# Two gaps of 128 bytes in on-chip memory, and four orders of the feed-forward's products

## The chip, the cores and the metric

The program runs on one core of a Trainium2 chip. The metric is device time in microseconds (us), from the first to the last instruction and a little around them; lower is better. The median of three runs of the kernel before is 1766.66 us.

## The reference

One layer of a hybrid diffusion backbone over 256 latent tokens and 256 context tokens of 2048 channels, in float32. What matters here is that nearly everything is a product of 256 (or 512) token rows with a large weight matrix:

```
h  = rmsnorm(x) * (1 + sc1) + sh1                    # and hc, of the context
na_q, na_k, na_v, dn_qkv, dn_z, ..., ft, sg_u, sg_v = split(h @ w_in)
y  = sum_i sigmoid(h @ w_gate[i] + b_gate[i]) * (branch_i @ w_branch[i])   # 4 branches
x  = x + g1 * (y @ w_out)
h  = rmsnorm(x) * (1 + sc2) + sh2
x  = x + g2 * ((silu(h @ w1) * (h @ w3)) @ w2)       # D_FF = 5632
```

## The kernel before

**Exact products in three parts.** A weight block of 256 rows and 512 columns (a "half block", two k tiles `j` = 0, 1 of 128 rows) arrives by DMA in a tile `raw`. ScalarE rounds it to float32r (`whi`, L392), VectorE forms the rest (`wlo = raw - whi`, L394). The activations are held as two such parts too: `hH`/`hL` (the normalised rows; later `h2H`/`h2L` in the same place), `hcH`/`hcL` (context), `yna`, `yft`, `yst`, `ydn` (branch outputs), `mT` and `m8` (the merged rows), `uH`/`uL` (feed-forward). A product is xH·whi + xL·whi + xH·wlo.

**One matmul.** `PE.matmul(acc, x, w)` takes 128x128 numbers of the activation as the stationary operand (the weight load, PEld LDWEIGHTS in the profile) and 128x512 numbers of `whi` or `wlo` as the moving one, and adds to `acc`, an accumulator in PSUM. Every matmul has its own load, so the stationary operand of the next matmul is read while the moving operand of this one streams.

**One half block.** `half_block` (L413 to L426) makes 12 matmuls: for the two token tiles in turn (two accumulators), xH with `whi` (j = 0, 1), xL with `whi` (0, 1), xH with `wlo` (0, 1). `half_blocks` (L442) does the same for a few half blocks with the token tiles outermost. The input projection's first part (L696) has its own loop, over latent tiles (`hH`) and context tiles (`hcH`) by turns.

**Stages.** Up to about 245 us: norms, modulation and the blocks that need the context (L696). Up to about 930 us: other projections, gates and branch products, with the mixers' small work in between. Up to about 1020 us: output projection (stationary `mT`, `m8`). Then the feed-forward: `w1`, `w3` (stationary `h2H`/`h2L`, 11 blocks `f`), and from 1513.5 us `w2` (stationary `uH`/`uL`, four column blocks `cbk`).

**What sets the order.** Class `Issue` merges lanes of side work into one program order around the weight stream, by a coarse model; `half_block` tells it of 0.64 us after each three matmuls (`iq.pe`). Every engine then issues in program order.

**Where tiles lie.** Pools are laid out in the order in which they are opened, each tile at an offset in bytes within a partition: `raw`, three `whi` of 4,096 bytes, three `wlo` of 4,096, the small tiles (1,024 in all), then the long-lived ones: `cb` (8,192), `hH`, `hL` (16,384 each), `kdn`, `vdn` (8,192 each), small ones (384 in all), and behind these the pools that come and go with the stages (`y8`, `hc`, `mT`, `u`). Slices of a tile by token tile, k tile or `j` start a multiple of 512 bytes into it.

Of the kernel before, what the change touches and what calls it, by code (L numbers as in the profile page):

```python
# [10 lines left out]
F32 = mybir.dt.float32  # L11
# [8 lines left out]
P = 128  # L20
D = 2048
T = 256
# [9 lines left out]
# columns of the packed per-channel parameters  # L32
C_BADA, C_N1, C_N2, C_CONV, C_QN, C_KN = 0, 96, 112, 128, 188, 189
NCOLS = 190
# columns of the constant matrices
M_ID, M_EF, M_EB, M_BD = (128 * i for i in range(4))
NMATS = 512
# how far ahead of its place in the program the weight stream is scheduled
AHEAD = 3000
CFG = {'cvpos': 3, 'cv': 0, 'qv': 0, 'dn': 0, 'ev': 2000, 'evp': 0, 'evx': 0, 'evf': 0, 'evA': 0, 'ahead': 3000, 'adahp': 0, 'proj': {7: 2, 4: 2, 5: 2, 6: 2, 8: 2, 9: 2}, 'gate': {2: 1, 3: 1, 0: 1, 1: 3}, 'wout': [4, 4, 4, 0], 'hopp': 0.2, 'hopb': 0.25, 'hop': 0.2, 'win': 0.5, 'eps': 0.1, 'nz': 1, 'ndn': 11, 'nout': 4, 'groups': [[0, 2], [2, 2], [4, 2], [6, 2], [8, 2], [10, 2], [12, 2], [14, 2]], 'pe': [1, 18], 'pa': 5, 'atail': 8, 'nproj': 2, 'ngate': [9, 0, 8], 'start': 'a0 s0 x0 x1 s1 a16 w0 a1 a17 x2 w1 x3 w2 w3 s2 s3 s4', 'px1': 2, 'psp': 3, 'hoppA': 0.25, 'winA': 0.5, 'winA0': 1, 'hopA': 0.1, 'cw': [0, 0], 'ph1': 1, 'pseed': 0, 'pevac': 1, 'slack': 0.5}  # L40
# groups of k tiles in which the first blocks of the input projection are accumulated
# [7 lines left out]
def _ada_on_pe(t):  # L49
    """Which tiles of the modulation matrix TensorE reduces (the others: VectorE)."""  # L50
    return t in PE_ADA


class Event:
    """A point of the program; t is its time in Issue's model once it has been reached."""
# [5 lines left out]
class Issue:  # L61
    """Merges lanes of work into one program order around the weight stream on TensorE.

    A lane is a generator. It yields, before an operation, the engine ("P", "V", "A" or "G") and about
    how long it holds it (for ScalarE also the function table), or ("wait", event), ("set", event) or
    ("delay", us). Operations are traced when a coarse model of the engines says that their inputs
    are there and their engine is free, so that no engine's queue is blocked by one that comes too early.
    """
# [74 lines left out]
    def stall(self, *events):  # L143
        """Trace other work until the events are reached."""
        for ev in events:
            for _ in range(100000):
                if ev.t is not None:
                    break
                self.now += 0.1
                self.pump()  # L150
            assert ev.t is not None
            while self.now < ev.t:
                self.now = min(ev.t, self.now + 0.3)
                self.pump()
# [10 lines left out]
def build(ctx, tc, A, dbg=None):  # L165
# [12 lines left out]
    hip = ctx.enter_context(pool("hi", 3))  # L178
    lop = ctx.enter_context(pool("lo", 3))
# [19 lines left out]
    def mean_rsqrt(out, in_, scale):  # L199
        """out = (scale * in_ + eps) ** -0.5"""  # L200
        S.activation(out, in_, AF.Sqrt, bias=epsc, scale=scale)
        V.reciprocal(out, out)

# [14 lines left out]
    first_inst = len(nc.cur_bb.bb.instructions)  # L218
    iq = Issue()
# [5 lines left out]
    def pin():  # L225
        """Every engine issues its instructions in program order."""
        last = {}
        for inst in list(nc.cur_bb.bb.instructions)[first_inst:]:
            if inst.engine in last:
                tc.add_manual_dep(inst, last[inst.engine], mybir.DependencyInfo(  # L230
                    mybir.DependencyClass.NoSync, mybir.DependencyReason.DATA), reason="program order")
            last[inst.engine] = inst.name
# [9 lines left out]
    # the stream from memory in the order of use: weights (by k tiles and blocks of 512 columns),  # L242
    # tiles of the modulation matrix in between
# [50 lines left out]
    state = {"k": 0}  # L294
# [108 lines left out]
    def acc_pair():  # L403
        """Two accumulators, and the events that their readers set."""
        res = []
        for _ in range(2):
            if len(accs_free) >= 4:
                iq.stall(accs_free[-4])
            accs_free.append(Event())
            res.append((acc_tile(), accs_free[-1]))  # L410
        return [r[0] for r in res], [r[1] for r in res]

    def half_block(accs, xs, kt0, start, stop, seeded=False):  # L413
        """accs[i] += x_i[:, kt0..]^T @ the next half block of the stream; xs: (hi, lo, token offset)."""
        k = state["k"]
        state["k"] += 1
        iq.stall(split_done[k])
        hi, lo = halves[k]
        for acc, (xh, xl, off) in zip(accs, xs):
            seq = [(xh, hi, j) for j in range(2)] + [(xl, hi, j) for j in range(2)] + [(xh, lo, j) for j in range(2)]  # L420
            for n, (xx, ww, j) in enumerate(seq):
                PE.matmul(acc, xx[:, kt0 + j, off:off + P], ww[:, j], start=start and n == 0 and not seeded,  # L422
                          stop=stop and n == 5, skip_group_check=seeded)
                if n % 3 == 2:
                    iq.pe(0.64)
        mm_done[k].t = iq.now  # L426

    def half_blocks(accs, xs, kts, n0, ready, done, cut=1):
        """Some half blocks from n0 on of an accumulation over eight, one accumulator after the other,
        the very last one in cut parts of its columns."""  # L430
# [80 lines left out]
    def c_lane():  # L511
        """silu(c) as columns, and on every partition as a row, for both streams."""
# [24 lines left out]
    def x_lane(s_, u):  # L537
        """One token tile, scaled to unit root mean square, in the groups of its use."""
# [38 lines left out]
    def mods_lane():  # L577
        """Shift and scale of the normalised rows, by k tile: h = (x * r) * a1 + sh."""
# [13 lines left out]
    def h_lane(s_, parts, banks):  # L592
        """The modulated rows, transposed, as exact float32r parts."""
# [29 lines left out]
    def seed_lane(gi, b, tt, slot):  # L623
        """The accumulator of one output tile; later groups of k tiles start from the sum so far."""
# [32 lines left out]
    # (block, half block, token tile, k tile in it); the first group by token tiles, as they arrive  # L657
# [26 lines left out]
    for gi, (k0, gn) in enumerate(GROUPS):  # L684
        k_first, n_q = state["k"], gn // 2
        state["k"] += 4 * n_q
        for b, q, tt, j in order[gi]:
# [17 lines left out]
            if (b, tt) == (0, 3) and last:  # L705
                # decay / beta columns: both parts of the weights beside each other
# [45 lines left out]
    # gated delta rule: convolutions, norms and decays  # L752
# [11 lines left out]
    def conv_head(src, h, ns, which, room):  # L764
        """Five-tap centred conv along the tokens, per stream, of one head; channels on partitions."""
# [33 lines left out]
    def decay_lane():  # L799
        # decays: g = -exp(a_log) * softplus(a + dt_bias), running sums inside a tile, per direction  # L800
# [35 lines left out]
        # the running sums as rows, for the differences between tokens  # L836
# [25 lines left out]
    # neighbourhood attention: every grid row is a key row (four rows, window of eight)  # L862
# [3 lines left out]
    def na_norm(src, n, dst, wc, x, done):  # L866
        """Root-mean-square norm over the head's channels, and the transpose."""
# [75 lines left out]
    # Fourier mixing  # L943
# [3 lines left out]
    def ft_lane():  # L947
# [9 lines left out]
        for g in range(4):  # L957
            # cosines of rows 0 .. T/2 and sines of rows 1 .. T/2 - 1; the other rows mirror them
# [22 lines left out]
    # spatial gating  # L981
# [48 lines left out]
    # blocks of 128 tokens: B'[j, i] = beta_j (k_j . k_i) exp(gc_i - gc_j), the masked q . k products  # L1030
    def dn_stage(dp):
# [24 lines left out]
        def qv_lane():  # L1056
            room = (lambda n: dp.tile([P, 2 * (T + 4)], F32, name=n, tag={"pad": "l20", "cv": "l21"}[n]), 1)
            # q stays unnormalised (its l2 factor scales the output rows)
# [65 lines left out]
        def sub_lane():  # L1124
            # inverses of the 32 x 32 diagonal blocks by substitution, one block a partition
# [42 lines left out]
        def level(d, tt):  # L1168
            """Blocks of 64, then 128:  V <- V - V (M o B') V"""
# [10 lines left out]
            # (first, second) blocks of a pair, in the order of the recurrence  # L1180
# [41 lines left out]
        # the scan, over tiles of 128 tokens: context first, then latent  # L1222
# [114 lines left out]
    def request_gate(key):  # L1337
        """Reserve the next two accumulators for a gate."""
        gate_waits[key] = accs_free[-4:-2]
        accs_free.extend((Event(), Event()))  # L1340
        gate_accs[key] = [None, accs_free[-2:]]
        gate_wanted[key].t = iq.now

    def bias_lane():
        """A gate's accumulators start from its bias."""
# [61 lines left out]
    def row_lane(dst, rows, m0, done):  # L1407
        """16 modulation columns as one row on every partition."""
# [71 lines left out]
    # gated rmsnorm of the delta rule's output  # L1480
# [115 lines left out]
    def xn_lane(tt):  # L1596
        """Rows of one token tile, scaled to unit root mean square."""
# [16 lines left out]
    def h2_lane(parts, b):  # L1614
        """The modulated rows, transposed, as exact float32r parts, by pairs of k tiles."""
# [24 lines left out]
    # half blocks that stay for both token tiles, one tile after the other  # L1640
# [56 lines left out]
    for f in range(NF):  # L1697
        u_done[f] = Event()
        a1_, f1 = acc_pair()
# [38 lines left out]
    for cbk in range(4):  # L1738
# [4 lines left out]
        xs = [(ff["uH"], ff["uL"], 0), (ff["uH"], ff["uL"], P)]  # L1743
        for f in range(NF):
# [14 lines left out]
def _blocks(w):  # L1759
    """[K, N] -> [N/512, K/512, 128, 4, 512]: each block is one contiguous load."""  # L1760
# [23 lines left out]
def _window():  # L1784
    """Additive column-window mask and the table positions of the attention bias."""
# [61 lines left out]
```

## Time and profile before

| | |
|---|---|
| three runs, us | 1766.38, 1766.66, 1768.25 |
| span of the profiled execution, us | 1764.7 |
| TensorE busy | 1716.4 us (97%), 8297 matmuls |
| VectorE, ScalarE, GpSimd busy | 69%, 54%, 8% |
| 128x512 matmuls with `whi`, `wlo` or `late` as moving operand | 6798 |

The profiled execution's own time outside its span is not listed; the runs lie 1.7 to 3.6 us over the span. [...]

### The profile page before, as it was taken

The numbers are of one execution on the slowest core, as the hardware profiler recorded it, in microseconds if no ns is written. First come the engines' busy times: TensorE is split into PE (matmuls) and PEld (weight loads), VectorE is DVE, ScalarE is ACT, GpSimd is POOL, SyncE is SP. The second block draws the span as 40 slices with busy tenths as digits, with TensorE's granted clock in tenths as the row PEclk, the third lists the DMA queues.
The fourth block names the chain that finished last, engine by engine and source line by source line (L and its number), as shares of the span: only waits on it lengthen the run. The fifth ranks groups of instructions, "written<-read, shape, count | busy, mean of one in ns | idle before, by whom it ended". The sixth has DMA issues, their size and how long they took to land.

```text
span 1764.7 us, 21765 instructions
## 1 busy us (share of the span) xinstructions
PE 1716.4 (97%) x8297; PEld 1398.3 (79%) x8297; DVE 1213.0 (69%) x1522; ACT 950.1 (54%) x1329; POOL 140.5 (8%) x136
## 2 busy tenths in 40 slices
PE   3999999999999999999999999999999999999998
PEld 2777888788778877988888878888888888888887
DVE  5899988885989865767877665565555555544444
ACT  5799987755556566235544474444444444333332
POOL 1000001100211153211101000000000000000000
PEclk9999999999999999999999999999999999999999
DMA  8677787657775755468777645666666655555552
GB/s 322 230 254 256 262 330 260 235 201 253 268 255 177 233 189 198 173 240 297 291 275 266 253 148 211 238 237 239 238 238 238 262 188 188 182 197 190 202 201 107
DMA packets 62461, 406.94 MB, mean 231 GB/s; under 512 B 7730, under 2 KB 8546, under 8 KB 16786
## 3 DMA queue, kind: packets, MB, share of 16 engines
q1 hardware_dynamic: 56164, 386.43, 59.8%
q0 software_dynamic: 4464, 16.49, 3.3%
q10 hardware_dynamic: 1728, 2.62, 0.4%
q8 instruction: 65, 1.06, 0.2%
q14 instruction: 40, 0.33, 0.0%
HBM read 401.29 MB, written 4.23 MB: 230 GB/s over the span
## 4 chain that ended last, share of the span: by engine, by line
PE 62%; issue 2%; POOL 1%; DMA 1%; ACT 0%; DVE 0%; POOLq 0%; ACTq 0%; DVEq 0%
PE acc L422 57%; PE acc L442 2%; POOL l L1175 1%; DMA raw<-w_gate 1%; PE ps L1692 1%; PE ps L1267 0%; POOL mg L1384 0%; PE ps L1256 0%; PE ps L1306 0%; PE ps L1209 0%; PE ps L1216 0%; PE ps L1278 0%; PE ps L1284 0%; PE ps L1288 0%; PE ps L1548 0%
## 5 line engine op out<-in xcount | busy, mean ns | idle before, releaser
L394 DVE TENSOR_TENSOR wlo<-raw,whi 128x1024 fp32r<-128x1024 f32 x532 | 667.0, 1256 | 429.2 <-ACT whi L392 425.6
L392 ACT CAST whi<-raw 128x1024 fp32r<-128x1024 f32 x532 | 558.6, 1052 | 583.9 <-PE acc L422 513.8
L422 PE MATMUL acc<-whi,hL 128*128 128x512 f32 x704 | 230.6, 398 | 0.0
L422 PE MATMUL acc<-whi,hH 128*128 128x512 f32 x704 | 224.5, 400 | 3.2 <-ACT acc L1359 2.6
L422 PE MATMUL acc<-wlo,hH 128*128 128x512 f32 x704 | 218.6, 392 | 2.9 <-DVE wlo L394 2.7
L422 PE MATMUL acc<-whi,h2L 128*128 128x512 f32 x684 | 213.5, 391 | 0.0
L422 PE MATMUL acc<-whi,h2H 128*128 128x512 f32 x684 | 211.7, 391 | 0.0
L422 PE MATMUL acc<-wlo,h2H 128*128 128x512 f32 x684 | 210.7, 389 | 0.0
L369 DVE SCALAR_TENSOR_TENSOR raw<-raw,cb 128x2048 f32<-128x2048 f32 x64 | 151.7, 2373 | 17.9 <-DMA raw<-w_ada 17.8
L422 PEld LDWEIGHTS acc<-wlo,hH 128*128 128x128 f32 x704 | 131.7, 188 | 32.6 <-DVE wlo L394 5.8
L422 PEld LDWEIGHTS acc<-whi,hL 128*128 128x128 f32 x704 | 132.4, 188 | 28.0 <-issue 0.7
L422 PEld LDWEIGHTS acc<-whi,hH 128*128 128x128 f32 x704 | 128.4, 189 | 30.1 <-ACT acc L1359 3.0
L422 PEld LDWEIGHTS acc<-wlo,h2H 128*128 128x128 f32 x684 | 128.4, 188 | 26.6
L422 PEld LDWEIGHTS acc<-whi,h2L 128*128 128x128 f32 x684 | 128.4, 188 | 26.6
L422 PEld LDWEIGHTS acc<-whi,h2H 128*128 128x128 f32 x684 | 127.6, 188 | 26.1
L422 PE MATMUL acc<-whi,uL 128*128 128x512 f32 x340 | 106.8, 395 | 0.0
L422 PE MATMUL acc<-whi,uH 128*128 128x512 f32 x340 | 106.7, 395 | 0.0
L422 PE MATMUL acc<-wlo,uH 128*128 128x512 f32 x340 | 106.5, 394 | 0.0
L357 DVE SCALAR_TENSOR_TENSOR junk<-raw,cb 128x2048 bf16<-128x2048 f32 x30 | 68.5, 2282 | 11.0 <-ACT cb L521 11.0
L422 PEld LDWEIGHTS acc<-whi,uL 128*128 128x128 f32 x340 | 64.1, 188 | 14.9
L422 PEld LDWEIGHTS acc<-wlo,uH 128*128 128x128 f32 x340 | 64.1, 188 | 14.9
L422 PEld LDWEIGHTS acc<-whi,uH 128*128 128x128 f32 x340 | 64.0, 188 | 14.9
(390 smaller groups left out, 2170.9 us busy)
## 6 DMA issues: line engine op xcount, KB each, us to landing
raw<-w SPq DMA_DIRECT2D x132, 1024.0 KB, 4.8
raw<-w_ada SPq DMA_DIRECT2D x96, 1024.0 KB, 5.9
raw<-w_gate SPq DMA_DIRECT2D x64, 1024.0 KB, 4.8
raw<-w_in SPq DMA_DIRECT2D x24, 1024.0 KB, 5.7
raw<-w_in SPq DMA_DIRECT2D x32, 512.0 KB, 5.4
raw<-w_branch SPq DMA_DIRECT2D x16, 1024.0 KB, 4.9
raw<-w_out SPq DMA_DIRECT2D x16, 1024.0 KB, 4.9
bg<-b_gate POOLq DMA_DIRECT2D x16, 256.0 KB, 4.3
```

The costliest lines, as they stand in the source:

```text
L357: V.scalar_tensor_tensor(junk, raw, 1.0, cb, ALU.mult, ALU.mult, accum_out=modA[:, 0, t:t + 1])
L369: V.scalar_tensor_tensor(raw, raw, 1.0, cb, ALU.mult, ALU.mult, accum_out=mod[:, t:t + 1])
L392: S.copy(hi, raws[e][:, 2 * q:2 * q + 2])
L394: V.tensor_tensor(lo, raws[e][:, 2 * q:2 * q + 2], hi.bitcast(F32), ALU.subtract)
L422: PE.matmul(acc, xx[:, kt0 + j, off:off + P], ww[:, j], start=start and n == 0 and not seeded, stop=stop and n == 5, skip_group_check=seeded)
L442: PE.matmul(acc[:, cs], xx[:, kt0 + j, off:off + P], ww[:, j, cs], start=n0 + n + i == 0, stop=n0 + n == 7 and i == 5, skip_group_check=c > 0)
L1175: G.tensor_tensor(dst.rearrange("p h (b i) -> p h b i", b=4), src[:, u0:u0 + 4].unsqueeze(2).to_broadcast([P, 4, 4, 32]), mats[:, M_BD:M_B ...
L1692: PE.transpose(tp[:, P * h:P * h + P], us[tt][:, P * h:P * h + P], ident)
```

## The change

Two tiles of 128 bytes, never written, are put into the layout: `gap0` between `whi` and `wlo`, `gap1` in front of the long-lived tiles. Everything behind them moves up. Offsets modulo 512 bytes, as the allocator gives them:

| tile | before | after |
|---|---|---|
| `raw`, `whi` | 384 | 384 |
| `wlo` | 384 | 0 |
| `hH`, `hL`, `h2H`, `h2L` | 384 | 128 |
| `hc`, `y` tiles, `m8`, `uH`, `uL` | 256 | 0 |
| `mT`, `late` | 160 | 416 |

In `half_block` the order of the 12 matmuls follows `state["mode"]`, which is 0 (the order before) until the feed-forward; there it is `f % 4` for `w1` and `w3` and `cbk` for `w2`. Mode 1 goes by j, with xH·whi, xH·wlo, xL·whi; mode 2 by j, with xH·whi, xL·whi, xH·wlo; mode 3 keeps the order of mode 0 but takes both accumulators in turn at each product. `half_blocks` is unchanged. Comments are removed as well, so L422 becomes L433, L1692 becomes L1703.

```
+    pad0 = ctx.enter_context(pool("pad0")).tile([P, 32], F32, name="gap0")
     lop = ctx.enter_context(pool("lo", 3))
...
+    pad1 = ctx.enter_context(pool("pad1")).tile([P, 32], F32, name="gap1")
     hp = ctx.enter_context(pool("h"))
...
-        for acc, (xh, xl, off) in zip(accs, xs):
-            seq = [(xh, hi, j) for j in range(2)] + [(xl, hi, j) for j in range(2)] + [(xh, lo, j) for j in range(2)]
-            for n, (xx, ww, j) in enumerate(seq):
-                PE.matmul(acc, xx[:, kt0 + j, off:off + P], ww[:, j], start=start and n == 0 and not seeded,
-                          stop=stop and n == 5, skip_group_check=seeded)
-                if n % 3 == 2:
-                    iq.pe(0.64)
+        mode = state.get("mode", 0)
+        seq = [(xh_, ww, j) for xh_, ww in ((0, hi), (1, hi), (0, lo)) for j in range(2)]
+        if mode == 1:
+            seq = [(xh_, ww, j) for j in range(2) for xh_, ww in ((0, hi), (0, lo), (1, hi))]
+        if mode == 2:
+            seq = [(xh_, ww, j) for j in range(2) for xh_, ww in ((0, hi), (1, hi), (0, lo))]
+        todo = [(a, n) for a in range(len(accs)) for n in range(6)]
+        if mode == 3:
+            todo = [(a, n) for n in range(6) for a in range(len(accs))]
+        for i, (a, n) in enumerate(todo):
+            which, ww, j = seq[n]
+            off = xs[a][2]
+            PE.matmul(accs[a], xs[a][which][:, kt0 + j, off:off + P], ww[:, j], start=start and n == 0 and not seeded,
+                      stop=stop and n == 5, skip_group_check=seeded)
+            if i % 3 == 2:
+                iq.pe(0.64)
...
     for f in range(NF):
         u_done[f] = Event()
+        state["mode"] = f % 4
...
         xs = [(ff["uH"], ff["uL"], 0), (ff["uH"], ff["uL"], P)]
+        state["mode"] = cbk
```

The numbers in the names of the next rows tell buffers apart (`acc_8924` and `acc_8925` are the two accumulators). TensorE, the third half block of `w1` at f = 1, before:

```order
L422 MATMUL acc_8924<-whi_8930,h2H_8421 128x512 x2
L422 MATMUL acc_8924<-whi_8930,h2L_8422 128x512 x2
L422 MATMUL acc_8924<-wlo_8931,h2H_8421 128x512 x2
L422 MATMUL acc_8925<-whi_8930,h2H_8421 128x512 x2
L422 MATMUL acc_8925<-whi_8930,h2L_8422 128x512 x2
L422 MATMUL acc_8925<-wlo_8931,h2H_8421 128x512 x2
```

The same half block after (mode 1):

```order
L433 MATMUL acc_8932<-whi_8938,h2H_8429 128x512
L433 MATMUL acc_8932<-wlo_8939,h2H_8429 128x512
L433 MATMUL acc_8932<-whi_8938,h2L_8430 128x512
L433 MATMUL acc_8932<-whi_8938,h2H_8429 128x512
L433 MATMUL acc_8932<-wlo_8939,h2H_8429 128x512
L433 MATMUL acc_8932<-whi_8938,h2L_8430 128x512
L433 MATMUL acc_8933<-whi_8938,h2H_8429 128x512
L433 MATMUL acc_8933<-wlo_8939,h2H_8429 128x512
L433 MATMUL acc_8933<-whi_8938,h2L_8430 128x512
```

`wlo` is now wanted by the second matmul, where it was the fifth, and `whi` and `wlo` follow each other more often. TensorE, a half block of `w2` in the last column block, before:

```order
L422 MATMUL acc_13096<-whi_13363,uH_8775 128x512 x2
L422 MATMUL acc_13096<-whi_13363,uL_8776 128x512 x2
L422 MATMUL acc_13096<-wlo_13364,uH_8775 128x512 x2
L422 MATMUL acc_13097<-whi_13363,uH_8775 128x512 x2
L422 MATMUL acc_13097<-whi_13363,uL_8776 128x512 x2
L422 MATMUL acc_13097<-wlo_13364,uH_8775 128x512 x2
```

The same half block after (mode 3):

```order
L433 MATMUL acc_13104<-whi_13371,uH_8783 128x512
L433 MATMUL acc_13105<-whi_13371,uH_8783 128x512
L433 MATMUL acc_13104<-whi_13371,uH_8783 128x512
L433 MATMUL acc_13105<-whi_13371,uH_8783 128x512
L433 MATMUL acc_13104<-whi_13371,uL_8784 128x512
L433 MATMUL acc_13105<-whi_13371,uL_8784 128x512
L433 MATMUL acc_13104<-whi_13371,uL_8784 128x512
L433 MATMUL acc_13105<-whi_13371,uL_8784 128x512
L433 MATMUL acc_13104<-wlo_13372,uH_8783 128x512
L433 MATMUL acc_13105<-wlo_13372,uH_8783 128x512
```

The accumulators take turns, and `whi` runs for eight matmuls, `wlo` for four. On TensorE nothing else changes place, and the other engines' instructions stand in the same order as before.

## Rows read from the trace of the kernel before

**Rows 1.** The page: span, busy time by engine, the chain that ended last.

```profile
span 1764.7 us, 21765 instructions
PE 1716.4 (97%) x8297; PEld 1398.3 (79%) x8297; DVE 1213.0 (69%) x1522; ACT 950.1 (54%) x1329; POOL 140.5 (8%) x136
...
PE acc L422 57%; PE acc L442 2%; POOL l L1175 1%; DMA raw<-w_gate 1%; PE ps L1692 1%; PE ps L1267 0%; POOL mg L1384 0%; PE ps L1256 0%; PE ps L1306 0%; PE ps L1209 0%; PE ps L1216 0%; PE ps L1278 0%; PE ps L1284 0%; PE ps L1288 0%; PE ps L1548 0%
```

**Rows 2.** The page's groups of matmuls: count | busy us, mean ns | idle us before.

```profile
L422 PE MATMUL acc<-whi,hH 128*128 128x512 f32 x704 | 224.5, 400 | 3.2 <-ACT acc L1359 2.6
L422 PE MATMUL acc<-whi,h2H 128*128 128x512 f32 x684 | 211.7, 391 | 0.0
```

**Rows 3.** Windows, L422 on TensorE: us, busy (matmuls), granted clock.

```profile
1165.00:1200.00 35.00, 35.00 (x156) 1.00 0.71 265
1650.00:1685.00 35.00, 35.00 (x152) 1.00 0.55 200
```

**Rows 4.** TensorE timeline: start us, length, tiles, matmuls; first and last rows of stretches.

```profile
46.53 0.39 PE L696 MATMUL acc<-wlo,hH 128*128 128x512 f32 x1
...
1164.80 0.61 PE L422 MATMUL acc<-wlo,h2H 128*128 128x512 f32 x2
...
1199.71 0.62 PE L422 MATMUL acc<-whi,h2L 128*128 128x512 f32 x2
...
1513.01 0.62 PE L422 MATMUL acc<-wlo,h2H 128*128 128x512 f32 x2
1513.47 0.64 PE L422 MATMUL acc<-whi,uH 128*128 128x512 f32 x2
1513.95 0.62 PE L422 MATMUL acc<-whi,uL 128*128 128x512 f32 x2
...
1519.93 0.62 PE L422 MATMUL acc<-whi,uH 128*128 128x512 f32 x2
...
1559.90 0.39 PE L422 MATMUL acc<-wlo,uH 128*128 128x512 f32 x1
```

**Rows 5.** Line L422, 1165 to 1200 us: count, duration ns min/median/max.

```profile
L422 PE MATMUL acc<-whi,h2H x52: 389/389/389, 1165.3 to 1199.5; 128*128 128x512 f32 x52
```

**Rows 6.** Line L422, 1525 to 1700 us.

```profile
L422 PE MATMUL acc<-wlo,uH x252: 390/393/404, 1525.0 to 1699.6; 128*128 128x512 f32 x126
```

**Rows 7.** Line L696, 200 to 250 us: latent and context by turns.

```profile
L696 PE MATMUL acc<-whi,hL x28: 387/389/398, 200.6 to 237.9; 128*128 128x512 f32 x28
L696 PE MATMUL acc<-whi,hcL x28: 390/393/404, 203.4 to 240.7; 128*128 128x512 f32 x28
```

**Rows 8.** Tiles mT and yft, 240 to 1100 us.

```profile
L422 PE MATMUL acc<-whi,mT x120: 392/395/483, 928.7 to 1004.2; 128*128 128x512 f32 x120
L422 PE MATMUL acc<-whi,yft x64: 390/395/481, 533.8 to 626.4; 128*128 128x512 f32 x64
```

**Rows 9.** Line L422, the one matmul at 796.2 us, at 1395.8 and at 333.2.

```profile
L422 PE MATMUL acc<-wlo,hH x1: 397/397/397, 796.0 to 796.0; 128*128 128x512 f32 x1
L422 PE MATMUL acc<-wlo,h2H x1: 388/388/388, 1395.6 to 1395.6; 128*128 128x512 f32 x1
L422 PE MATMUL acc<-wlo,hH x1: 400/400/400, 333.0 to 333.0; 128*128 128x512 f32 x1
```

**Rows 10.** Line L711: loads and matmuls of a stationary tile used twice running.

```profile
L711 PEld LDWEIGHTS ps<-hH,wabr x16: 187/188/192, 59.6 to 223.1; 128*128 128x128 f32 x16
L711 PEld LDWEIGHTS ps<-hL,wabr x16: 187/188/189, 59.8 to 223.2; 128*128 128x128 f32 x16
```

**Rows 11.** Timelines of VectorE and TensorE: wlo, the feed-forward's u, its transposes.

```profile
1155.60 1.23 DVE L394 TENSOR_TENSOR wlo<-raw,whi 128x1024 fp32r<-128x1024 f32 x1 [1.50 <-ACT whi L392]
1156.75 0.68 DVE L1686 TENSOR_TENSOR us<-us,acc 128x512 f32<-128x512 f32 x1
...
1159.54 0.60 PE L1692 MATMUL ps<-mats,us 128*128 128x128 f32 x4
```

**Rows 12.** Waits of TensorE, 250 to 1513 us: for whom, us, times, longest.

```profile
PE acc L422 <- DVE wlo L394: 2.7, 3, 1.6
```

## The prediction, made before the changed kernel ran

> **What bounds the kernel now.** I read the page's head first: TensorE is busy 97% of the span, and one line, the matmul of the half blocks (L422), makes 57% of the chain that ended last [rows 1]. VectorE and ScalarE have room. From 250 us to the end of w3 the longest single cause for which TensorE waits is `wlo`, 2.7 us in three waits [rows 12]. So the time is the number of matmuls times their pace, and the change touches nothing else: no engine gets an instruction more or less, and only TensorE's order differs.
>
> The pace is read from start to start. In a quiet stretch of w1 and w3, 154 matmuls lie between the rows at 1164.80 and 1199.71 us: 34.91 / 154 = 226.7 ns each. In w2, 172 lie between 1519.93 and 1559.90: 39.97 / 172 = 232.4 ns [rows 4]. [...] The change comes at one point: pairs start 0.45 us apart until `uH` takes the place of `h2H`, and 0.48 us apart with the first pair of w2 [rows 4]. The durations show it matmul by matmul: 389 ns each time with `h2H` [rows 5], 390 to 404 with `uH` [rows 6]. It isn't the stage: in the first part latent and context tiles alternate, and the median is 389 with `hL` and 393 with `hcL`, under the same `whi` [rows 7]. With `mT` and `yft` no matmul is below 390, the medians are 395 [rows 8].
>
> What these tiles differ in is where they lie. I call **distance** the offset of the next stationary tile minus that of the moving one, modulo 512 bytes, since the next weights are read while this matmul streams. From the layout's table: `h` and `h2` have 0 against `whi` and `wlo` alike, context, branch and `u` tiles and `m8` 384, `mT` 288. Distance 0 is the quiet pace, 384 and 288 are not. Slices start a multiple of 512 bytes into a tile, so the distance doesn't change inside a tile.
>
> **The change part by part.**
>
> *The gaps.* They shift `wlo` by 128 bytes and all behind it by 256. The new distances: `h` tiles 256 against `whi` and 128 against `wlo`; context, branch, `u` tiles and `m8` 128 against `whi` and 0 against `wlo`; `mT` 32 and 416; the `late` tiles as before. No `h` tile is at 0 any more. Which of the new distances stalls?
>
> For 256 one row speaks: at 796.2 us a small weight load at distance 256 (16 columns of `mod`) follows a quiet stretch, and the matmul over it takes 397 ns, 8 over the quiet 389; the same instruction at 1395.8 us, at distance 448, leaves its matmul at 388 [rows 9]. So 256 stalls, by one sample and a short load. For 128 there is no row. Its neighbours are 0 (nothing) and 192, where the one at 333.2 us takes 400 ns, 11 over [rows 9]. The bounds for 128 are thus 0 and 11 ns; I take it as stalling, at the sustained 5.7 ns, since all the full-width cases off 0 that run on for long (288 and 384) do [rows 6, 8].
>
> The sum, then. The matmuls with `h` stationary are 3 x 704 and 3 x 684 at L422 [rows 2] and 384 at L696. Of them 3,380 now run at the quiet pace, counted as those whose successor starts 226 or 227 ns later, the first at 46.53 us, the last at 1513.01 [rows 4]; 1,665 of these are in w1 and w3. The others stand behind transposes and small work and are off that pace already. 3,380 x 5.7 ns = 19.3 us lost, if all go to w2's pace. Its spread: if only the two thirds with `whi` pay, 12.9 us; at `mT`'s pace (median 395, 6 over 389) it is 3,380 x 6.5 = 22 us. TensorE waits little after 250 us [rows 12], so nearly all of this is on the path; I take 1 us off for waits on side lanes that get shorter.
>
> What comes back: 1,910 matmuls with context, branch, `u` and `m8` tiles pay 5.7 ns now, 10.9 us in all, 1,034 of them in w2. After the change a third of them, those over `wlo`, are at 0. But a stalled stretch doesn't turn quiet at once: behind the switch from context to latent tiles the first few still take more than 389, up to 398 [rows 7], and with two `wlo` matmuls at a time (one in modes 1 and 2, four in mode 3) there is hardly a stretch long enough. I put it at 0, bounds 0 and 3.6 us gained.
>
> *The orders.* (a) They could change the pace only through the switches from `whi` to `wlo`; that is in the numbers above. (b) Mode 1 has the same stationary tile twice running, 280 times. At L711, where that happens now, each matmul has a load of its own, 16 and 16 [rows 10]; so no load falls away, and 0. (c) Mode 3 changes the accumulator with every matmul. Now it changes with every sixth, and in the quiet stretch all 52 are at 389 [rows 5]: 0, both ways. (d) Modes 1 and 2 want `wlo` three matmuls earlier at most, 0.7 us. VectorE makes it in 1.23 us, itself waiting for ScalarE's `whi` [rows 11], and L422 waits for it three times only, none in the feed-forward [rows 12]: the third buffer hides this. Without that cover it would be 0.7 us a half block, but I see no such place. (e) In mode 3 the first accumulator of a pair is done five matmuls later, 1.1 us. VectorE's product `us` started at 1156.75 us and took 0.68 [rows 11]; its transposes stood at 1159.54 [rows 11], 2.1 us after its end, so 1 us is left: 0.
>
> *VectorE* reads `raw` and `whi`, unmoved, and writes `wlo` 128 bytes further. No row shows it with `wlo` elsewhere. I take 0; 10% either way (0.12 of the 1.23 us, [rows 11]) is far less than the room under (d), and VectorE is 69% busy in all [rows 1].
>
> [...]
>
> **The rivals.**
> 1. *Offsets are not the cause* (some other property of the tiles decides). Then all stays, 1766.7. For it: distance and tile go together in this trace, so a property of the tile would look the same. Against: `hc` and `hH` are made by the same code and differ by place alone. 11%. [...]
> 2. *Faster: both 128 and 256 are quiet.* What stalls might be only a band around 288 to 384. Then `h` keeps its pace, and the 1,910 others come down to it: 1766.7 - 10.9 = 1755.8. It decides in w2, where 1,034 x 5.7 = 5.9 us of it lie: the point is whether `uH` over `whi`, at 128, starts 227 ns apart. Against: the 397 at distance 256. 12%.
> 3. *128 is quiet, 256 is not.* `u`, branch and context tiles become quiet altogether (-10.9), `h` pays over `whi` (+12.9 to +19.3): 1769 to 1775. 12%.
> 4. *Worse: each switch between `whi` and `wlo` sets the pace back*, and the matmuls pay the 11 ns of the single sample at 192 rather than 5.7: 3,380 x 11 = 37 us, 1804. 5%.
>
> **How the numbers follow.** The forecast (60%) is that `h` loses its quiet pace and the others don't gain: 1766.7 + 19.3 - 1 = 1785 us, about 1,783 on the profile's own span of 1764.7. Its own range is 1779 to 1789 (the 12.9 and 22 us from above). Rivals 1 and 3 (23%) lie below, and with them the range reaches from 1764 to 1792; out of it are rival 2, rival 4 and a little of the forecast, about 19%. A difference of 0.2% (3.5 us) is about what a measurement of this kernel can tell from none. Faster: rival 2, 12%. The same: rival 1, 11%. Slower: the forecast, rivals 3 and 4, 77%.
>
> **What would show it.** In the changed kernel's trace: matmuls with `h2H` of w1 and w3 at 390 to 404 rather than 389, pairs 0.465 us apart; w2 as now, about 232 ns; f = 0, 1, 2, 3 alike within 1 ns; no new wait of TensorE. If w1 and w3 stand at 389, I am wrong on 256 (rival 2) or on the cause (rival 1), and w2's durations tell which: 389 there is rival 2, 393 is rival 1. If w2 alone is quiet, it is rival 3. If the four modes differ by more than 2 ns, the switches matter by themselves, and rival 4 or a gain that I have left out is at work.

## The result, and the profile after

The changed kernel takes 1776.65 us (median of four runs, 1774.91 to 1784.58) against 1766.52 for the kernel before beside it: a ratio of 1.0075, with a 95% interval of 1.0051 to 1.0100. It is slower, by 10.1 us on the median and by 8.4 us between the two profiled executions (spans 1773.1 and 1764.7). The page of the changed kernel, to be held against [rows 1] and [rows 2] (span; busy us, share, count; then groups with busy us and mean ns of one):

```profile
span 1773.1 us, 21729 instructions
PE 1725.7 (97%) x8297; PEld 1395.4 (79%) x8297; DVE 1212.4 (68%) x1522; ACT 949.7 (54%) x1329; POOL 139.4 (8%) x136
...
L433 PE MATMUL acc<-whi,h2H 128*128 128x512 f32 x684 | 240.7, 395 | 0.0
...
L433 PE MATMUL acc<-whi,hH 128*128 128x512 f32 x704 | 226.6, 403 | 2.2 <-ACT acc L1370 2.0
...
L433 PE MATMUL acc<-wlo,uH 128*128 128x512 f32 x340 | 116.7, 391 | 0.0
```

The same 8297 matmuls keep TensorE busy 9.3 us longer. The groups with `h2H` and `hH` went from 391 and 400 ns to 395 and 403. (The busy times of the `h2H` group, 211.7 and 240.7 us, can't be compared: overlaps count once within a group, and in the new orders its matmuls seldom follow each other.) VectorE, ScalarE and GpSimd did as much as before. Windows with the matmuls of L433 (us, busy, count, granted clock, DMA share, GB/s), for [rows 3]:

```profile
1165.00:1200.00 35.00, 34.81 (x151) 1.00 0.61 229
1650.00:1685.00 35.00, 35.00 (x155) 1.00 0.55 200
```

In 35 us of w1 and w3 now 151 matmuls run where 156 did, and in w2 155 where 152 did, at a granted clock of 1.00 in all four. TensorE's waits from 250 us to the end of w3 (for whom, us, times, longest), for [rows 12]:

```profile
PE ps L1197 <- POOL l L1186: 3.6, 3, 1.8
PE ps L942 <- DVE rc L937: 2.5, 1, 2.5
PE acc L433 <- ACT acc L1370: 2.0, 1, 2.0
PE acc L433 <- DVE wlo L396: 1.2, 1, 1.2
```

No new wait came; the one for `wlo` fell from 2.7 to 1.2 us, and the one for `l` rose from 2.7 to 3.6. So the loss has to lie in the pace of the matmuls.

**The pace, block by block.** In the quiet stretch of the kernel before, rows 389 ns long start 226.7 ns apart [rows 4, 5], so neighbours overlap; what a matmul costs is read from start to start. These are single rows of the changed kernel's TensorE timeline (start us, length), the first and the last of a stretch of f = 2, of f = 7 and of the second column block of w2, in this order:

```profile
1130.11 0.39 PE L433 MATMUL acc<-whi,h2H 128*128 128x512 f32 x1
...
1158.11 0.39 PE L433 MATMUL acc<-whi,h2H 128*128 128x512 f32 x1
...
1350.04 1.07 PE L433 MATMUL acc<-whi,h2L 128*128 128x512 f32 x4
...
1383.08 1.07 PE L433 MATMUL acc<-whi,h2L 128*128 128x512 f32 x4
...
1600.03 0.39 PE L433 MATMUL acc<-wlo,uH 128*128 128x512 f32 x1
...
1639.17 0.39 PE L433 MATMUL acc<-wlo,uH 128*128 128x512 f32 x1
```

Between them lie 120, 144 and 171 matmuls: 28.00 / 120 = 233.3 ns, 33.04 / 144 = 229.4 and 39.14 / 171 = 228.9. Read so for every block (the mean from start to start of matmuls that follow each other within 260 ns; the kernel before has 227.0 in w1 and w3 by this measure, where its quiet stretch alone has the 226.7 of [rows 4], and 232.4 in w2):

| | mode 0 | mode 1 | mode 2 | mode 3 |
|---|---|---|---|---|
| w1, w3 | 231.3, 231.2, 231.1 (f = 0, 4, 8) | 231.1, 231.1, 231.1 (1, 5, 9) | 233.2, 231.2, 233.2 (2, 6, 10) | 231.3, 229.5 (3, 7) |
| w2 | 231.9 | 229.0 | 229.0 | 232.2 |

Summed over the trace, matmul by matmul against the kernel before: `h` of the first and the middle part (2,203 matmuls) +6.85 us, `h2` (2,052) +8.90, context tiles -0.68, branch tiles -0.35, `u` -1.98, `mT` and `m8` 0.0, and the spaces around waits and small work (all that starts later than 260 ns, or isn't a matmul of this shape), nearly all ahead of the feed-forward, -4.45. Together +8.3 of the 8.4 us.

### The profile page after: what moved, and what is told of

Same layout as the page of the kernel before. It is cut to its first block, busy times and chain, and to the rows that moved or that the text cites. A ratio compares the mean times of both kernels' runs of the same rounds, so it can differ in the third digit from the quotient of the medians.

```text
span 1773.1 us, 21729 instructions
## 1 busy us (share of the span) xinstructions
PE 1725.7 (97%) x8297; PEld 1395.4 (79%) x8297; DVE 1212.4 (68%) x1522; ACT 949.7 (54%) x1329; POOL 139.4 (8%) x136
## 4 chain that ended last, share of the span: by engine, by line
PE 62%; issue 2%; POOL 1%; DMA 1%; ACT 0%; DVE 0%; POOLq 0%; ACTq 0%
PE acc L433 57%; PE acc L453 2%; POOL l L1186 1%; DMA raw<-w_gate 1%; PE ps L1703 1%; PE ps L1278 0%; POOL mg L1395 0%; PE ps L1267 0%; PE ps L1317 0%; PE ps L1220 0%; PE ps L1227 0%; PE ps L1295 0%; PE ps L1289 0%; PE ps L1299 0%; PE ps L1559 0%
## 5 line engine op out<-in xcount | busy, mean ns | idle before, releaser
L433 PE MATMUL acc<-whi,h2L 128*128 128x512 f32 x684 | 240.9, 394 | 0.0
L433 PE MATMUL acc<-whi,h2H 128*128 128x512 f32 x684 | 240.7, 395 | 0.0
L433 PE MATMUL acc<-wlo,h2H 128*128 128x512 f32 x684 | 239.9, 393 | 0.0
L433 PE MATMUL acc<-whi,hL 128*128 128x512 f32 x704 | 232.5, 401 | 0.0
L433 PE MATMUL acc<-whi,hH 128*128 128x512 f32 x704 | 226.6, 403 | 2.2 <-ACT acc L1370 2.0
L433 PE MATMUL acc<-wlo,hH 128*128 128x512 f32 x704 | 220.5, 394 | 1.3 <-DVE wlo L396 1.2
L433 PEld LDWEIGHTS acc<-wlo,hH 128*128 128x128 f32 x704 | 132.3, 188 | 31.7 <-DVE wlo L396 2.8
L433 PEld LDWEIGHTS acc<-whi,hL 128*128 128x128 f32 x704 | 132.8, 189 | 30.1 <-issue 0.7
L433 PEld LDWEIGHTS acc<-whi,hH 128*128 128x128 f32 x704 | 128.3, 188 | 31.3 <-ACT acc L1370 2.4
L433 PEld LDWEIGHTS acc<-whi,h2H 128*128 128x128 f32 x684 | 128.1, 188 | 29.6
L433 PEld LDWEIGHTS acc<-whi,h2L 128*128 128x128 f32 x684 | 128.3, 188 | 29.3
L433 PEld LDWEIGHTS acc<-wlo,h2H 128*128 128x128 f32 x684 | 128.3, 188 | 29.0
L433 PE MATMUL acc<-whi,uL 128*128 128x512 f32 x340 | 117.6, 393 | 0.0
L433 PE MATMUL acc<-whi,uH 128*128 128x512 f32 x340 | 117.2, 393 | 0.0
L433 PE MATMUL acc<-wlo,uH 128*128 128x512 f32 x340 | 116.7, 391 | 0.0
L433 PEld LDWEIGHTS acc<-wlo,uH 128*128 128x128 f32 x340 | 63.8, 188 | 14.5
L433 PEld LDWEIGHTS acc<-whi,uL 128*128 128x128 f32 x340 | 63.9, 188 | 14.4
L433 PEld LDWEIGHTS acc<-whi,uH 128*128 128x128 f32 x340 | 63.7, 188 | 14.5
```

The lines of the kernel that those rows point to most:

```text
L433: PE.matmul(accs[a], xs[a][which][:, kt0 + j, off:off + P], ww[:, j], start=start and n == 0 and not seeded, stop=stop and n == 5, skip_gr ...
```

## The experiments

Distance is used as in the prediction: the offset of the next stationary tile minus that of the moving one. In each of these kernels the whole computation is done. Ratios stand against the kernel before on the same chip.

**One part alone: the four orders** (both gaps taken out of the changed kernel).

```
-    pad0 = ctx.enter_context(pool("pad0")).tile([P, 32], F32, name="gap0")
-    pad1 = ctx.enter_context(pool("pad1")).tile([P, 32], F32, name="gap1")
```

> The four orders in the feed-forward alone, no gaps: every distance is as in the kernel before (0 for h and h2, 384 for u). Distance theory: an order that doesn't change the distance does nothing; w1 and w3 start every 226.7 ns for all f, w2 every 232.4 ns for all four cbk; 1766.5 us, within 3 us. Rival (the orders cost by themselves: the same stationary tile twice running in mode 1, the accumulator changed at each matmul in mode 3): f = 2, 6, 10 at up to 233 ns as in the changed kernel, w1 and w3 some 8 us longer in all, 1770 to 1775 us.

1765.77 us against 1765.76, ratio 0.9999 (0.9983 to 1.0015). w1 and w3 stand at 227.0 ns in every f, whatever its mode, and w2 at 232.4 in all four column blocks. From 1165 to 1200 us, which [rows 5] show in the kernel before (the few longer ones stand around transposes):

```profile
L431 PE MATMUL acc<-whi,h2H x52: 387/389/398, 1164.6 to 1198.4; 128*128 128x512 f32 x52
```

At the constant distances of the kernel before the order costs nothing, and neither `wlo` wanted earlier nor the change of accumulators shows.

**The other part alone: the gaps** (both `state["mode"]` lines taken out).

> The two gaps alone, the order before everywhere. Distance theory: all of w1 and w3 at what f = 0, 4, 8 show in the changed kernel (231.2 ns), all of w2 at what cbk = 0 shows (231.9 ns rather than a mean of 230.5): the changed kernel's time plus 1 to 2 us, 1776 to 1780 us. Rival (the orders make the loss): w1 and w3 at 226.7 ns, at most 1768 us.

1774.92 us, ratio 1.0070 (1.0042 to 1.0097): all of the loss, 1 us under the range that I had expected. w1 and w3 stand at 231.2 in every f, w2 at 231.8 in every column block. From 1165 to 1200 us:

```profile
L433 PE MATMUL acc<-whi,h2H x52: 388/394/473, 1164.8 to 1199.8; 128*128 128x512 f32 x52
```

**The absolute offset or the distance?** A gap in front of `raw` moves every tile by 128 bytes and leaves all distances.

```
+    pada = ctx.enter_context(pool("pada")).tile([P, 32], F32, name="gapa")
     rawp = ctx.enter_context(pool("raw", 3))
```

> 128 bytes in front of raw, so that raw, whi, wlo and everything behind move up together: every offset is new, every distance is that of the kernel before. Distance theory: nothing changes, w1 and w3 at 226.7 ns, w2 at 232.4 ns, span near 1765 us. Rival (the offset of the stationary tile decides, quiet at 384 modulo 512 only): w1 and w3 leave 226.7 ns, as h2 is now at 0.

227.0 to 227.1 and 232.4 ns, as before. The time was 1767.77 in one execution, and 1761.91 for the kernel before beside it, whose executions lie between 1761.3 and 1770.9; so single times say little here, and the paces say it. That all tiles lie 128 bytes further does nothing; how they lie to each other is what counts.

**Every distance 0.** 128 bytes behind the small long-lived tiles bring context, branch and `u` tiles to distance 0, 96 more bring `mT` there; `wlo` and `h` stay.

```
     ab = hp.tile([P, 4, 16], F32, name="ab")
+    padu = hp.tile([P, 32], F32, name="gapu")
...
     dsm = sc.enter_context(pool("dsm"))
+    padm = dsm.tile([P, 24], F32, name="gapm")
```

> The kernel before with 128 bytes behind the h tiles and 96 in front of the merge's tiles, so that every stationary tile (context, branch, u, m8, mT) is at distance 0 from whi and wlo, and h stays there. Distance theory: all quiet stretches at 226.7 ns; 1,910 x 5.7 ns and 190 x 6.4 ns come off, 12 us: 1754.5 us (1752 to 1757). Rival (another property of these tiles makes them slow): w2 stays at 232.4 ns, 1766.5 us.

1753.97 us against 1765.76, ratio 0.9935 (0.9913 to 0.9958). It beats both kernels. Line of the half blocks in w2, 1650 to 1685 us (count, ns min/median/max), where [rows 6] has 390/393/404:

```profile
L423 PE MATMUL acc<-whi,uL x52: 389/389/389, 1649.7 to 1683.9; 128*128 128x512 f32 x52
L423 PE MATMUL acc<-wlo,uH x52: 389/389/389, 1650.1 to 1684.4; 128*128 128x512 f32 x52
```

`u` gained 5.84 us, branch tiles 1.80, context 1.62, `mT` 1.20, `m8` 0.98: 11.4 of the 12.5 us by which its span is shorter (1752.2). The prediction's 10.9 us for these tiles was about right, and the cause, distance, is shown by a gain as well as by a loss. The same matmuls of w2 run at 226.7 ns here and at 232.4 in the kernel before, at a granted clock of 1.00 in both (1535 to 1700 us). By what path the offset acts no run shows.

One more rival: `raw` lies at `whi`'s offset modulo 512, so the party that disturbs could be the transfers into `raw`. The end of w2 in the kernel before speaks against it (us, TensorE busy and count, granted clock, DMA share, GB/s):

```profile
1700.00:1710.00 10.00, 10.00 (x44) 1.00 0.64 238
...
1740.00:1748.00 8.00, 8.00 (x36) 1.00 0.09 36
```

With transfers at 0.64 and at 0.09 of the time the pace is 232.4 ns in both.

**The second gap alone, at four sizes.** `wlo` stays, all long-lived tiles move, so `h` has one distance against `whi` and `wlo` alike. The edit, with 128 bytes, is the diff's `gap1` line; for the others the tile has 64, 48 or 16 elements for 256, 192 and 64 bytes.

> Only the second gap (128 bytes in front of the long-lived tiles), the order before: h and h2 at 128 from whi and wlo alike, context, branch, u and m8 at 0. Distance theory with 128 a stalling distance: w2 at 226.7 ns (-10.9 us with the context and branch tiles), w1 and w3 at 230 to 232.5 ns (+13 to +19 us, less what waits take up): 1768 to 1775 us. Rival (only the alternation of two distances stalls, a constant 128 is quiet): w1 and w3 at 226.7 ns, 1755 us.

128 bytes: 1776.62 us, ratio 1.0064 (1.0045 to 1.0084), 1.6 us over the range that I had expected. `h` and `h2` lost 9.54 + 11.71 = 21.25 us, `u` gained 5.84. The blocks of w1 and w3 show two rhythms for one code and one distance: 233.2 or 233.3 ns for f = 0, 2, 4, 6 and 9, 232.4 for f = 1, 3, 5, 7 and 10 (f = 8 has 232.6). Of f = 3 and f = 4, in this order:

```profile
L423 PE MATMUL acc<-wlo,h2H x50: 390/392/404, 1165.0 to 1199.6; 128*128 128x512 f32 x50
...
L423 PE MATMUL acc<-wlo,h2H x49: 387/396/398, 1210.8 to 1245.2; 128*128 128x512 f32 x49
```

> Only the second gap, 256 bytes wide: h and h2 at a constant 256, context, branch, u and m8 at a constant 128. Theory (every distance but 0 modulo 512 stalls): w1 and w3 at 231 to 233.5 ns; w2 at 232.4 or 233.2 ns, the two paces that h2 showed at 128 with the second gap alone; span 1778 to 1785 us. Rival (the measure is modulo 256, so that 256 is as good as 0, which the 226 ns intervals over whi in the changed kernel's f = 7 suggest): w1 and w3 at 226.7 ns, span near 1765 us.

256 bytes: w1 and w3 stay at 227.0 ns, w2 at 232.4; 1763.33 us in one execution, beside 1761.91. From 1165 to 1200 us:

```profile
L423 PE MATMUL acc<-whi,h2H x52: 389/389/389, 1164.8 to 1199.0; 128*128 128x512 f32 x52
L423 PE MATMUL acc<-whi,h2L x52: 389/389/389, 1165.2 to 1199.5; 128*128 128x512 f32 x52
L423 PE MATMUL acc<-wlo,h2H x52: 389/389/389, 1165.7 to 1199.9; 128*128 128x512 f32 x52
```

These are [rows 5] again, at distance 256. My theory that 256 stalls fell, and its rival, that only the distance modulo 256 counts, came out.

> The second gap, 192 bytes wide: h and h2 at 192, u at 64. Theory (every distance but 0 stalls): both at 230 to 234 ns, span 1778 to 1785 us. Rival (a band around 0 is quiet, 64 in it): w2 at 226.7 ns and w1, w3 slower.

192 bytes: 1768.53 us; `h2` at 192 runs at 228.95 ns, `u` at 64 (modulo 256) at 233.3.

> The second gap, 64 bytes wide: h and h2 at 64, u at 448, which is 64 on the other side of 0. Theory (every distance but 0 stalls): both at 230 to 234 ns, span 1778 to 1785 us. Rival (a band of 64 bytes on either side of 0 is quiet): w1, w3 and w2 all at 226.7 ns, span 1754 us. One-sided: only one of the two is quiet.

64 bytes: 1786.15 us, the slowest of all; `h2` at 64 runs at 233.3 ns, `u` at 192 at 228.9. The roles are exchanged and the paces go with the distance. In both, the tile at 192 is faster than the 230 to 234 ns that I had expected of every distance but 0, and 64 bytes are no quiet band around 0. Durations over `wlo` in both kernels, 1165 to 1200 us, 192 bytes first:

```profile
L423 PE MATMUL acc<-wlo,h2H x50: 388/390/392, 1165.7 to 1198.9; 128*128 128x512 f32 x50
```

```profile
L423 PE MATMUL acc<-wlo,h2H x50: 393/398/405, 1165.1 to 1199.8; 128*128 128x512 f32 x50
```

The map so far, for a stretch in which the distance is constant:

| distance modulo 256 | 0 | 32 | 64 | 96 | 128 | 160 | 192 | 224 |
|---|---|---|---|---|---|---|---|---|
| ns from start to start | 226.7 | 233.1 | 233.3 | 234.2 | 232.4 or 233.2 | 233.4 | 228.9 | 233.3 |
| seen with | `h`, `u` | `mT` | `h`, `u` | `mT` | `h`, `u` | `mT` | `h`, `u` | `mT` |

The values at 96, 160 and 224 are those of `mT` (some 180 matmuls each) in the traces with 64, 128 and 192 bytes. Of all steps of 32 bytes only 0 and 192 are off the slow pace, and 224, nearer to 0 than 192, is on it.

**The first gap alone.** This has the mixed distances of the changed kernel with the roles exchanged: `h` at 128 over `whi` and 0 over `wlo`, `u` at 0 over `whi` and 128 over `wlo`.

```
+    pad0 = ctx.enter_context(pool("pad0")).tile([P, 32], F32, name="gap0")
     lop = ctx.enter_context(pool("lo", 3))
```

> The first gap alone, order as before: wlo and all behind it move by 128 bytes. Distances modulo 256: h tiles 128 over whi and 0 over wlo, context, branch and u tiles and m8 0 over whi and 128 over wlo; the shares of the changed kernel with the roles of h and u exchanged. If the pace follows from the distances of a run of matmuls, whatever tile it is: w1 and w3 at 231.8 ns (the gaps alone have that in w2, where two thirds are at 128 and one third at 0), w2 at 231.2 (theirs in w1 and w3); h loses 3,380 x 5.0 = 17 us, u and its like gain 1,910 x 1.1 = 2 us, about 1780 against 1765. If each matmul paid for its own distance alone: w1 and w3 at 230.5, w2 at 228.6, and 1772.

1776.92 us against 1766.62. w1 and w3 run at 231.8 or 231.9 ns in every f, w2 at 231.1 or 231.2: the paces of the gaps alone, exchanged, so which tile it is doesn't matter, and a matmul doesn't pay for its own distance alone. From 1165 to 1200 us, over `wlo` (distance 0 now) and over `whi` (128):

```profile
L423 PE MATMUL acc<-wlo,h2H x50: 388/395/398, 1164.8 to 1198.9; 128*128 128x512 f32 x50
L423 PE MATMUL acc<-whi,h2H x50: 392/393/479, 1165.3 to 1199.3; 128*128 128x512 f32 x50
```

The matmuls over `wlo` are at distance 0 and yet slower than those at 128: a third or two thirds of quiet distances don't make a quiet stretch. The time lies 3 us under the 1780 that I had expected; `h` lost the 17 us as expected, and the spaces around small work ahead of the feed-forward shrank by 5.0 us in this execution, a term that scatters (see the account of the waits below).

**What the orders do where distances mix.** The changed kernel once more, and both gaps with one order throughout (`state["mode"] = 1`, or 3, at both places).

> The changed kernel once more, for the steadiness of what its trace showed. If the pace follows from distances and order alone, the blocks of w1 and w3 read as in the first trace, one by one: f = 2 and 10 at 233.2 ns from start to start, f = 6, which has the same code and the same distances, at 231.2, f = 7 at 229.5 and f = 3 at 231.3; w2 at 231.9, 229.0, 229.0 and 232.2 in its four column blocks; time 1775. If instead a block settles into one of several rhythms by how it begins, the mean of a mode stays within 229 to 233.5, but the blocks of one mode differ again and not the same ones as before: any of f = 2, 6, 10 may stand at 231.2 or 233.2, and w2's second and third column blocks may leave 229.0; time 1772 to 1780.

Block by block the second execution repeats the first within 0.1 ns: f = 2 and 10 at 233.2, f = 6 at 231.2, f = 7 at 229.5, w2 at 231.9, 229.0, 229.0 and 232.2. So the difference between f = 2 and f = 6, one code and the same distances, isn't chance. (Its time, 1782.26, has another cause, told in the last section.)

> Both gaps, and order 1 in every block of the feed-forward. If the order decides the pace where distances mix: w1 and w3 at 231.1 ns in every f (as f = 1, 5, 9 of the changed kernel), w2 at 229.0 in all four column blocks (as its second one); against the gaps alone (231.2 and 231.8 ns) that is 1,034 x 2.8 ns = 2.9 us less, 1772. If blocks choose their rhythm by how they begin: some f at 233.2 and some column blocks at 231.8, and a time within 2 us of the gaps alone, 1775.

1772.95 us. w1 and w3 at 231.0 to 231.2, w2 at 228.9 to 229.1 in all four column blocks, 2.9 ns under the gaps alone: `u` gained 3.55 us against the kernel before. The sequence has a steady beat of three, of the moving operands `whi`, `wlo` and `whi` (here in w2, 1710 to 1745 us):

```profile
L433 PE MATMUL acc<-whi,uL x52: 391/391/391, 1709.6 to 1744.6; 128*128 128x512 f32 x52
L433 PE MATMUL acc<-whi,uH x52: 393/393/393, 1709.8 to 1744.9; 128*128 128x512 f32 x52
L433 PE MATMUL acc<-wlo,uH x51: 388/388/388, 1710.1 to 1744.4; 128*128 128x512 f32 x51
```

> Both gaps, and order 3 (whi for eight matmuls, wlo for four) in every block of the feed-forward. If the order decides the pace: w1 and w3 alike in every f, at 231.3 or 229.5 ns (the changed kernel's f = 3 and f = 7), w2 at 232.2 in all four column blocks; 1771 to 1775. If blocks choose their rhythm by how they begin: w1 and w3 again show both 231.3 and 229.5 in one run. A third view, that a matmul pays for its own distance alone and order is nothing, would have two thirds at 226.7 and a third at 232.4, 228.6 on the mean for w1 and w3.

1776.1 us. w1 and w3 at 231.4 or 231.5 in every f from 1 on (within 0.2 ns of the changed kernel's f = 3, and 1.9 off its f = 7), w2 at 231.7 in all column blocks; the time lies 1 us over the expected range. With both gaps and one order throughout the blocks agree; in the changed kernel, where the orders alternate, a block of mode 3 stands at 231.3, 229.5 or 232.2. So where distances mix a block's order alone doesn't fix its pace. That what ran before it decides is likely and not shown: f = 2 and f = 6 both follow a block of mode 1 and differ. The view that each matmul pays for its own distance alone (228.6 for w1 and w3) fell here too.

## Why the prediction was right or wrong

The forecast had the right sign and the right cause, and its size was too large: 1785.0, with +19 us, against 1776.65 and +10.1. Point by point:

- **TensorE's pace is the time, and distance sets the pace: right.** The loss is in the gaps alone (1.0070 of 1.0075), and none of it in the orders alone (0.9999). Rival 1, another property of the tiles, fell with every distance at 0, where the same tiles become quiet (w2 at 226.7 ns); the gap in front of all tiles can't speak against it, but shows that the absolute offset is not the cause.
- **"So 256 stalls, by one sample and a short load": wrong, and this is the step that failed.** With 256 bytes all matmuls of the half blocks from 1165 to 1200 us stand at 389, and w1 and w3 at 227.0 ns throughout. The 397 ns of [rows 9] belong to one matmul with a load of 16 columns; it says nothing of full loads. The distance counts modulo 256, not modulo 512: 0 and 256, 128 and 384, 192 and 448 give the same paces (227.0, 232.4 and 228.9 ns, and 233.2 in some blocks at 128).
- **128 stalls, at 5.7 ns: right.** Constant 128 gives 232.4 or 233.2, 5.7 or 6.5 ns over quiet, the forecast's value and the one that I had taken for `mT`'s. Rivals 2 and 3, in which 128 was quiet, fell. What the forecast described, all of `h` stalled, is the second gap of 128 bytes alone: 21.25 us, against the forecast's 19.3 and its upper end of 22.
- **The term of `h`: 19.3 us forecast, 15.75 measured** (6.85 + 8.90). Not all `h` matmuls are at a stalling distance, as I thought, but one third, those over `wlo`. By their own distance alone they would cost a third of 21.25, 7.1 us. The rest, 8.7 us, is the mixture: stalled and quiet distances in turn give 231.2, nearer to the stalled pace than to the quiet one. That a stretch doesn't turn quiet at once, the argument by which I took the gain of `u` as 0, holds for `h` as well. That the term came within 4 us is luck: the mixture, which the sum had for `u` and not for `h`, hides most of the first mistake. (The 1,665 matmuls given for w1 and w3 are 1,870 by the trace; the sum uses the 3,380, which hold.)
- **What comes back: 0 forecast, bounds 0 to 3.6; measured 3.0 us** (0.68 + 0.35 + 1.98). 2.0 of it is `u`, and most of that comes from modes 1 and 2 in w2; with the gaps alone `u` gains 0.55.
- **Waits: 1 us off forecast, 4.45 measured** in spaces ahead of the feed-forward. The waits that the trace names fell by less than 2 us. The same term is +3.35 for the orders alone, +0.47 for the gap in front of all and -3.8 for 256 bytes, whose paces are those of before, so it scatters by some 7 us from one execution to another; in the kernels with a loss in `h` it lies between -7.5 and +2.3. Of the 4.45, 1.3 us lie before 50 us and 1.3 between 245 and 320, where the granted clock stood at 0.50 for some 7 and some 3 us longer in the profiled execution of the kernel before (last section). How much of the rest belongs to the change stays open.
- **The orders: 0 forecast for (b) to (e), and that is shown** by the orders alone (ratio 0.9999). For (a), the switches, I had the place but no term. In the changed kernel the blocks differ by up to 3.7 ns (229.5 to 233.2), more than the 2 ns that I had named as the sign that switches matter by themselves. Rival 4 had `h` pay 11 ns a matmul for them; they cost nothing at a constant distance, and at mixed distances they move a block both ways. Against the gaps alone, `h2` lost 0.5 us more and `u` gained 1.4 more, which the times can't tell from 0 (1776.65 and 1774.92).

What stays open is how a stretch of mixed distances chooses its rhythm, as in f = 2 and f = 6, why constant 128 has two rhythms, and by what path the offsets act.

## What to carry to other kernels

When one engine is busy 97% of the time, compare the pace of one shape in different stretches of the same trace before looking at waits: 5.7 ns in 232 were 11.4 us here. On a kernel whose matmuls each load new stationary data (only float32r ones of 512 columns were measured here), lay the stationary and the moving tiles a multiple of 256 bytes apart (at 0 and at 256 w1 and w3 ran at 227.0 ns here; every distance at 0 was worth 0.65%, for 224 bytes of padding), and keep that distance for all moving operands of a loop, since mixtures of 0 and 128 ran at 229.0 to 233.2 ns here, most of them near the stalled pace. A single odd matmul in an otherwise quiet stretch, above all of another shape, is no sample of a sustained pace: the 397 ns at 256 stood 8 over the quiet 389, and stretches at 256 ran at the quiet pace.

## What was not expected of the hardware

**Distances modulo 256 bytes set the matmul's spacing.** Matmuls of 512 columns with a new load each started 226.7 ns apart at distance 0, 228.9 at 192 and 232.4 to 234.2 at the other six of the map. A distance of 192 costs only 2.2 ns and one of 64 costs 6.6, so the two directions aren't alike at 64 bytes; at 32 bytes both cost 6.4 to 6.6. The single matmul of [rows 9] at 192 was 11 ns over the quiet 389, while a sustained stretch at 192 loses 2.2: one stall among quiet matmuls is no measure for many.

**The rhythm is steady and repeats.** Two executions of the changed kernel agree in every block within 0.1 ns, 233.2 and 231.2 for equal code included.

**The granted clock falls in some executions and not in others, and that moves the times.** In the second execution of the changed kernel TensorE's timeline (length, tiles, matmuls, idle time before and who ended it) shows a wait of 1.86 us at 640 us, and the matmuls behind it take 1.22 us a pair, where a pair ahead of it took 0.63:

```profile
636.43 0.63 PE L433 MATMUL acc<-whi,hH 128*128 128x512 f32 x2
...
640.79 0.64 PE L1197 MATMUL ps<-l,Bm 32*32 32x32 f32 x16 [1.86 <-POOL l L1186]
641.36 1.22 PE L433 MATMUL acc<-whi,hH 128*128 128x512 f32 x2
```

Windows of the same execution (us, TensorE busy and count, granted clock, DMA share, GB/s):

```profile
640.00:644.00 4.00, 3.21 (x22) 0.53 0.63 188
644.00:648.00 4.00, 4.00 (x34) 0.50 0.56 233
648.00:652.00 4.00, 4.00 (x28) 0.50 0.00 0
652.00:656.00 4.00, 4.00 (x22) 0.77 0.00 0
656.00:660.00 4.00, 4.00 (x51) 1.00 0.30 72
```

From 640 to about 654 us the granted clock stood at 0.50, and from 648 to 656 us nothing was transferred. Against the first execution this one lay 1.8 us behind at 625 us and 7.5 us behind at 694: 5.7 us lost, most of the 7.4 us by which its span is longer. A wait of 1.8 us for the same work stands in the first execution too, and there the clock stayed at 1.00; what decides between the two is not shown here.

It isn't the only fall. Windows of the kernel before, then two of the changed kernel's first execution, in this order:

```profile
312.00:315.00 3.00, 3.00 (x13) 0.52 0.77 251
```

```profile
312.00:315.00 3.00, 3.00 (x23) 1.00 0.88 287
508.00:511.00 3.00, 3.00 (x8) 0.50 0.84 305
```

These two falls came behind waits of 2.4 and 2.0 us; a wait of 2.5 us at 311 us in the changed kernel brought none. The execution with 256 bytes stood at 1.00 from 50 us to 1760. In the 20 us from 630 on, the spaces grew against the kernel before by 5.2 to 6.6 us in the three executions that had some 10 us or more at 0.50 there (orders alone, 64 bytes, changed kernel's second), by 1.4 to 2.5 in the four that had some 3 us, and by at most 1.0 in the other six. So differences of a few us between single times are no sign of the change, and the paces at a granted clock of 1.00 are.
